# A depthwise convolution of 31 taps, with two more of its eight channel tiles on TensorE

## The chip, the cores and the metric

The kernel runs on one core of a Trainium2 chip. The metric is the device time of one execution in microseconds, as the median of several runs. TensorE (PE) multiplies matrices into PSUM, VectorE (DVE), ScalarE (ACT) and GpSimd (POOL) work elementwise, and SyncE (SP) issues most of the DMAs.

## The reference, cut to what matters

Two transformer blocks are computed in fp32 on a sequence of 512 positions of width 1024. The change lies in the convolution layer that opens the second block:

```python
def conformer_conv(x, norm_g, pw1_w, pw1_b, dw_w, dw_b, ln_g, ln_b, pw2_w, pw2_b):
    a, b = jnp.split(rmsnorm(x, norm_g) @ pw1_w + pw1_b, 2, axis=-1)
    h = a * jax.nn.sigmoid(b)
    h = lax.conv_general_dilated(h, dw_w[:, None, :], window_strides=(1,),
        padding=[(CONV_WIDTH - 1, 0)], feature_group_count=h.shape[-1], ...) + dw_b
    h = jax.nn.silu(layernorm(h, ln_g, ln_b))
    return h @ pw2_w + pw2_b
```

A first projection gives 2048 columns, whose halves are gated into 1024 channels. Each channel is filtered along the sequence by 31 taps of its own (causal: position s reads s-30 to s). Then come a layer norm over the channels, a SiLU and a second projection of 1024 columns.

## The kernel before

Activations lie transposed: a tile is 128 channels by 512 positions, so a layer has eight channel tiles, c = 0 to 7. The stage has four kinds of work.

**First projection.** `dense_g` (L259) makes one output tile after the other. Each fp32 product is three matmuls (`prod`, L228), with operands and weights split into a high and a low part; a tile takes 8 steps of 3 matmuls. Its weights come by DMA (`p_r`, SP's queue), are rounded on ACT (`p_h`, L223), and the rest is formed on DVE (`p_l`, L225). The opening group makes four tiles (the gates and values of c = 0 and 1) and lies before the code that is changed; twelve tiles follow, gate and value in turn for c = 2 to 7. A finished tile is read out of PSUM by DVE: a gate at L1196 (tile `sg`, then a sigmoid on ACT), a value at L1201 and L1202 (tile `gl`, the gated result). These products have three PSUM banks (`psm`), so a tile can't begin before the third one ahead of it has been read out.

**Filter on the elementwise engines** (`conv_taps`, L1259). On DVE a channel tile takes one multiplication (L1270) and 30 multiply-adds, one for each further tap (L1277, tile `dw`). With `two` set, ACT makes the 30 products instead (tile `dt`) and POOL adds them up (L1275). Before the change tiles 0 and 2 go the first way, one after the other, and tile 1 the second.

**Filter on TensorE** (`conv_start`, L1215, and `conv_pe`, L1243). Tiles 3 to 7 go this way. POOL builds two tiles `bd` of block-diagonal weights (L1223) from constants and taps alone. Four tiles `x4` hold shifted copies of the channel tile: 8 copies on ACT (L1236), 8 DMAs from SP's queue (L1238), after 4 small memsets on DVE (L1232). Then 8 groups of 4 matmuls, each 32 output columns wide, add up the taps (L1249). DVE reads the result out (L1254). For the last two tiles, 6 and 7, the same matmuls are in `close` (L1323), half of the sequence at a time, and DVE reads them out in `squares` (L1332, L1336).

**Layer norm.** After tile 0 is filtered, a matmul with ones takes its mean over 128 channels (L1288, tile `lnk`). This is subtracted from every tile to keep the sums of squares small. Each tile is added to a sum (L1303) and its square to another (L472). In `seam` (L300) the order is: `close(0)`, `squares(0)`, eight steps of `close(1)`, the statistics of the first half, its operands, the rest of `close(1)`, and so on; the second projection then begins. Because tile 6 has one PSUM bank, `close(1)` waits until `squares(0)` has read it.

**Order.** The streams are put in order by `Mix` (L88), with a clock of its own. A stream yields the time that it occupies TensorE and a delay until its next turn; among those that are ready the lowest rank goes first. The tap streams have rank 0 and 1, `conv_start` 10 + c, the projection 40 (0.65 for each step) and `conv_pe` 50. Only the projection, `lnk` and `conv_pe` move the clock, and `conv_pe` gets no turn before the projection is through. Each engine works its instructions off in one order fixed when the program is built. Activations share a pool of 72 slots.

Of the kernel before, what the change touches and what calls it, by code (L numbers as in the profile page):

```python
# [28 lines left out]
CMP = 31  # L29
NG = 8  # L30

C_PE, C_GP = 3, 1


C_ID, C_TRI, C_DM, C_LV = 0, 128, 256, 512
# [90 lines left out]
def body(ctx, tc, I, out, dump=None):  # L126
# [11 lines left out]
    def slot(name, dt=F32):  # L138
        return act.tile([P, S], dt, tag="s", name=name)
# [7 lines left out]
    def bank(name):  # L147
        return psg.tile([P, S], F32, tag="g", name=name)
# [16 lines left out]
    def af(o, i, func, **k):  # L165
        if func in (AF.Ln, AF.Exp):
            lnexp()
        elif func not in (AF.Copy, AF.Square):
            table[0] = func
        return A.activation(o, i, func, **k)  # L170
# [783 lines left out]
    mix = Mix()  # L954
# [299 lines left out]
            V.scalar_tensor_tensor(acc, ps, dwb[:, c:c + 1], sums["k"], ALU.add, ALU.subtract)  # L1254
            centred(c, acc)

    first = min(c for c in range(C_PE) if c != C_GP)

    def conv_taps(c, two, tap):  # L1259

        yield lambda: c in glu
        if two:
            yield 0.0, 16
        acc, t = slot(f"dw{c}"), glu[c]
        w = lambda d: dww[:, c, d:d + 1]
        if two:
            tmp = [slot(f"dt{c}_{i}") for i in range(5)]
            af(acc, t, AF.Identity, scale=w(0), bias=dwb[:, c:c + 1])
        else:
            V.tensor_scalar(acc, t, w(0), dwb[:, c:c + 1], ALU.mult, ALU.add)  # L1270
        for d in range(1, 31):
            if two:
                x = tmp[d % 5]
                af(x[:, d:], t[:, 0:S - d], AF.Copy, scale=w(d))
                G.tensor_tensor(acc[:, d:], acc[:, d:], x[:, d:], ALU.add)  # L1275
            else:
                V.scalar_tensor_tensor(acc[:, d:], t[:, 0:S - d], w(d), acc[:, d:], ALU.mult, ALU.add)  # L1277
            yield 0.0, tap
        return acc

    def conv_dve(two, cs, tap):
        for c in cs:
            acc = yield from conv_taps(c, two, tap)
            if c == first:

                yield 0.0, 4
                pk = bank("lnk")
                T.matmul(pk, ones, acc, start=True, stop=True)  # L1288
                k = slot("lnk")
                af(k, pk, AF.Copy, scale=1.0 / P)  # L1290
                sums["k"] = k
                yield 0.86, 1.25
            V.tensor_tensor(acc, acc, sums["k"], ALU.subtract)
            centred(c, acc)

    def centred(c, acc):
        cv[c] = acc
        if "s" not in sums:
            sums["s"] = slot("lns")
            V.tensor_copy(sums["s"], acc)  # L1300
            sums["q"] = Sq("lnq")
        else:
            V.tensor_tensor(sums["s"], sums["s"], acc, ALU.add)  # L1303
        sums["q"].add(acc)

    mix = Mix()
    mix.add(conv_dve(False, [c for c in range(C_PE) if c != C_GP], 1.2), 0)
    mix.add(conv_dve(True, [C_GP], 2), 1)
    for c in range(C_PE, KD):
        mix.add(conv_start(c), 10 + c)  # L1310
    mix.add(dense_g("p1", xs, pw1_groups, evacs["p1"], skip=1), 40)
# [377 lines left out]
    mix = Mix(2.5)  # L1689
# [108 lines left out]
```

## Time and profile before

| | |
|---|---|
| median of 3 runs (lowest, highest) | 2069.87 us (2067.83, 2072.08) |
| the profiled execution: time, span | 2069.71 us, 2067.9 us |
| PE busy | 1979.4 us, 96% of the span |
| DVE busy | 1575.2 us, 76% |
| ACT busy | 1032.5 us, 50% |
| POOL busy | 322.4 us, 16% |
| mean granted TensorE clock | 0.987 |

The time is that of the whole execution, and the span runs from the first to the last instruction. Shares are over the whole span; the convolution stage is about 130 us of it, from 893 to 1025 us.

### The profile page before, as it was taken

What the parts mean: (1) busy time and instruction counts of PE and PEld (TensorE: products, weight loads), DVE (VectorE), ACT (ScalarE), POOL (GpSimd) and SP (SyncE); (2) the same over time, 40 slices, a digit from 0 to 9 for tenths busy, and PEclk for the clock granted to TensorE, in tenths of its full rate; (3) what the DMA queues carried; (4) which work ended last, traced back from release to release, by engine and by line L of the source; (5) the groups of instructions that cost most, each with busy time, mean ns of one, the idle gap of its engine ahead of it and who ended that gap; (6) DMA issues with size and microseconds to landing.
All of it is one profiled execution on the core that took longest, in us unless ns stands there. A gap on an engine that the chain in (4) does not pass through costs nothing.

```text
span 2067.9 us, 31921 instructions
## 1 busy us (share of the span) xinstructions
PE 1979.4 (96%) x12400; PEld 1695.1 (82%) x12400; DVE 1575.2 (76%) x2914; ACT 1032.5 (50%) x1726; POOL 322.4 (16%) x225
## 2 busy tenths in 40 slices
PE   7898889999999999997799999999999999999998
PEld 5777777878899988885488999888766678999987
DVE  5888888655989972599978999634888868999832
ACT  5545666553544452456564445424756644444522
POOL 3332433101100000257000000000233310000000
PEclk9999999999999999998999999999999999999999
DMA  5221112312223333222122333324100022323332
GB/s 148 62 56 47 52 52 72 133 61 82 91 83 110 97 122 96 81 82 82 52 92 82 103 103 113 112 92 125 52 22 21 22 62 72 112 96 120 105 95 66
DMA packets 204190, 171.91 MB, mean 83 GB/s; under 512 B 13121, under 2 KB 198858, under 8 KB 204040
## 3 DMA queue, kind: packets, MB, share of 16 engines
q1 hardware_dynamic: 196864, 163.33, 25.5%
q10 hardware_dynamic: 6152, 3.40, 0.6%
q0 software_dynamic: 1024, 3.15, 0.4%
q8 instruction: 98, 1.61, 0.3%
q14 instruction: 52, 0.43, 0.1%
HBM read 165.15 MB, written 2.10 MB: 81 GB/s over the span
## 4 chain that ended last, share of the span: by engine, by line
PE 76%; DVE 18%; ACT 3%; issue 2%; DMA 1%; POOL 0%; ACTq 0%; DVEq 0%; SPq 0%; POOLq 0%
PE f L230 16%; PE f L232 16%; PE f L231 16%; DVE dw L1277 2%; PE ao L1676 2%; PE pT L1655 2%; DVE br L727 1%; DVE xc L728 1%; PE s L1568 1%; PE wo L230 1%; PE wo L232 1%; PE wo L231 1%; PE s L1566 1%; DVE p_l L225 1%; PE p L231 1%
## 5 line engine op out<-in xcount | busy, mean ns | idle before, releaser
L225 DVE TENSOR_TENSOR f_l<-f_r,f_h 128x1024 fp32r<-128x1024 f32 (+2 forms) x88 | 101.0, 1149 | 166.8 <-ACT f_h L223 166.3
L223 ACT CAST f_h<-f_r 128x1024 fp32r<-128x1024 f32 (+2 forms) x88 | 87.1, 992 | 188.4 <-PE f L231 148.7
L1646 POOL TENSOR_SCALAR p<-p,dn 128x256 f32<-128x256 f32 (+2 forms) x64 | 73.9, 1159 | 119.5 <-DVE dn L1644 87.3
L170 ACT ACTIVATE p<-s,nm 128x512 f32<-128x512 f32 (+3 forms) x128 | 66.2, 527 | 34.8 <-DVE nm L1640 13.9
L1442 POOL CAST KB<-K 128x128 fp32r<-128x128 f32 x4 | 1.6, 411 | 473.1 <-ACT K L1418 473.1
L1277 DVE SCALAR_TENSOR_TENSOR dw<-gl,dww,dw 128x511 f32<-128x511 f32 (+29 forms) x60 | 64.1, 1068 | 1.0
L170 ACT ACT_TABLE_LOAD x45 | 57.7, 1283 | 12.8 <-DVE v L644 4.9
L359 DVE TENSOR_TENSOR f_s<-f_s,f 128x1024 f32<-128x1024 f32 x52 | 63.3, 1218 | 0.1
L225 POOL TENSOR_TENSOR p_a_l<-p_a_r,p_a_h 128x1024 fp32r<-128x1024 f32 x4 | 9.9, 2474 | 330.3 <-DMA p_a_r<-in_a_pw_w 315.4
L1640 DVE TENSOR_REDUCE nm<-s 128x1 f32<-128x512 f32 (+2 forms) x96 | 50.1, 546 | 7.4 <-PE s L1568 6.7
L354 ACT CAST f_q1h<-f 128x1024 fp32r<-128x1024 f32 x26 | 27.3, 1051 | 55.8 <-DVE f_q3l L355 55.0
L1275 POOL TENSOR_TENSOR dw<-dw,dt 128x511 f32<-128x511 f32 (+29 forms) x30 | 47.1, 1571 | 33.0 <-ACT dt L170 31.1
L355 DVE TENSOR_TENSOR f_q1l<-f,f_q1h 128x1024 fp32r<-128x1024 f32 x26 | 31.9, 1225 | 24.9 <-ACT f_q1h L354 24.9
L1655 PEld LDWEIGHTS pT<-cst,p 128*128 128x128 f32 x320 | 36.0, 140 | 9.1 <-issue 4.2
L1676 PE MATMUL ao<-pt,vN 128*64 128x128 f32 (+3 forms) x256 | 42.6, 440 | 0.0
L354 ACT CAST f_q7h<-f 128x1024 fp32r<-128x1024 f32 x26 | 27.3, 1050 | 29.1 <-DVE f_q2l L355 26.6
L1655 PE MATMUL pT<-cst,p 128*128 128x128 f32 x320 | 41.0, 274 | 0.2 <-DVE pt L1659 0.2
L354 ACT CAST f_q2h<-f 128x1024 fp32r<-128x1024 f32 x26 | 27.4, 1054 | 27.6 <-issue 25.8
L727 DVE TENSOR_TENSOR br<-br,uc 128x4 f32<-128x4 f32 (+14 forms) x120 | 38.6, 321 | 2.5
L354 ACT CAST f_q5h<-f_s 128x1024 fp32r<-128x1024 f32 x26 | 27.3, 1052 | 26.3 <-DVE f_s L359 25.6
L354 ACT CAST f_q6h<-f_s 128x1024 fp32r<-128x1024 f32 x26 | 27.4, 1055 | 25.9 <-DVE f_s L359 21.5
L728 DVE TENSOR_TENSOR xc<-xc,br 128x4 f32<-128x4 f32 (+14 forms) x120 | 37.1, 309 | 2.7
(2420 smaller groups left out, 7963.2 us busy)
## 6 DMA issues: line engine op xcount, KB each, us to landing
f<-in_ffn_w_in SPq DMA_DIRECT2D x72, 512.0 KB, 3.9
f<-in_w_ffn_in SPq DMA_DIRECT2D x32, 512.0 KB, 3.5
f_r<-in_ffn_w_out SPq DMA_DIRECT2D x30, 512.0 KB, 3.4
p_r<-in_a_pw_w SPq DMA_DIRECT2D x20, 512.0 KB, 3.9
f_r<-in_w_ffn_out SPq DMA_DIRECT2D x14, 512.0 KB, 3.5
wo_r<-in_w_out SPq DMA_DIRECT2D x12, 512.0 KB, 3.4
f_r<-in_ffn_w_out SPq DMA_DIRECT2D x14, 384.0 KB, 3.1
wk_r<-in_gdn_w_in SPq DMA_DIRECT2D x8, 512.0 KB, 3.7
```

The source lines that it names most:

```text
L170: return A.activation(o, i, func, **k)
L223: A.copy(hi, raw)
L225: (G if idle else V).tensor_tensor(lo, raw, hi.bitcast(F32), ALU.subtract)
L230: T.matmul(ps, wh, xh, start=first, stop=False)
L231: T.matmul(ps, wh, xl, start=False, stop=False)
L232: T.matmul(ps, wl, xh, start=False, stop=last)
L354: A.copy(hi, raw)
L359: V.tensor_tensor(raws[o], raws[a], raws[b], ALU.add)
L1277: V.scalar_tensor_tensor(acc[:, d:], t[:, 0:S - d], w(d), acc[:, d:], ALU.mult, ALU.add)
L1646: (V if br else G).tensor_scalar(pp[br, qb], pp[br, qb], den[:, br:br + 1], None, ALU.mult)
L1655: T.transpose(ps[:, off + (qb - kb) * P:off + (qb - kb + 1) * P], bl(pp[br, qb], kb), ident)
L1676: T.matmul(po[64 * i:64 * i + 64, kb * P:S], VN[br][:, kb * P + 64 * g:kb * P + 64 * g + 64], rhs, start=False, stop=j == 7)
```

## The change

The constant that says how many tiles the elementwise engines filter goes from 3 to 1, and the one that names ACT's and POOL's tile goes. Only tile 0 stays, on DVE. Tiles 1 and 2 join tiles 3 to 5 in the loops over `range(C_PE, KD)` of `conv_start` and over `range(C_PE, KD - 2)` of `conv_pe`. The delay for a tap goes from 1.2 to 1.1. The branch for `two` stays in the code without a caller.

```diff
-C_PE, C_GP = 3, 1
+C_PE = 1
...
-    first = min(c for c in range(C_PE) if c != C_GP)
+    first = 0
...
     mix = Mix()
-    mix.add(conv_dve(False, [c for c in range(C_PE) if c != C_GP], 1.2), 0)
-    mix.add(conv_dve(True, [C_GP], 2), 1)
+    mix.add(conv_dve(False, range(C_PE), 1.1), 0)
     for c in range(C_PE, KD):
         mix.add(conv_start(c), 10 + c)
```

## Rows read from the trace of the kernel before

**Rows 1.** The page, part 1: engine, busy us (share), instructions.

```profile
PE 1979.4 (96%) x12400; PEld 1695.1 (82%) x12400; DVE 1575.2 (76%) x2914; ACT 1032.5 (50%) x1726; POOL 322.4 (16%) x225
```

**Rows 2.** Busy time by stretch: us, engines (instructions), granted clock, DMA.

```profile
893.06:936.80 43.74, 43.71 (x194) 35.86 (x192) 43.40 (x49) 23.09 (x32) 23.04 (x15) 1.00 0.37 107
936.80:954.10 17.30, 5.23 (x11) 3.39 (x12) 17.19 (x17) 7.71 (x12) 16.53 (x11) 0.58 0.21 65
954.10:975.59 21.49, 21.49 (x90) 17.02 (x88) 18.01 (x22) 17.47 (x29) 10.58 (x7) 0.94 0.37 98
975.59:995.65 20.06, 20.06 (x193) 6.26 (x196) 19.85 (x29) 13.67 (x22) 10.62 (x7) 1.00 0.31 89
995.65:1003.06 7.41, 7.41 (x132) 4.44 (x124) 7.22 (x11) 4.04 (x6) 0.00 (x0) 1.00 0.45 123
1003.06:1013.38 10.32, 0.00 (x1) 0.00 (x1) 10.12 (x17) 2.32 (x5) 0.00 (x0) 0.73 0.16 51
1013.38:1025.08 11.70, 10.61 (x133) 5.29 (x133) 7.64 (x20) 6.56 (x13) 0.00 (x0) 0.80 0.00 1
```

**Rows 3.** Waits of PE, 890 to 1030: us in total, times, longest.

```profile
PE cv L1328 <- DVE dw L1336: 10.3, 1, 10.3
PE lnk L1288 <- DVE x L1232: 8.6, 1, 8.6
PE p L230 <- DVE gl L1201: 3.5, 1, 3.5
```

**Rows 4.** PE in order of time, 890 to 1026: start, us, line, count, [idle before].

```profile
893.06 0.40 PE L230 MATMUL p<-f2x0h,p_h 128*128 128x512 f32 x1
...
931.17 0.39 PE L230 MATMUL p<-f2x0h,p_h 128*128 128x512 f32 x1
...
953.05 2.05 PE L1288 MATMUL lnk<-dw,ones 128*128 128x512 f32 x2 [8.59 <-DVE x L1232]
...
975.59 20.25 PE L1249 MATMUL cv<-x,bd 128*32 128x512 f32 x192
995.65 7.41 PE L1328 MATMUL cv<-x,bd 128*32 128x256 f32 x128
1013.38 5.96 PE L1328 MATMUL cv<-x,bd 128*32 128x256 f32 x64 [10.32 <-DVE dw L1336]
...
1020.33 3.66 PE L1328 MATMUL cv<-x,bd 128*32 128x256 f32 x64
```

**Rows 5.** DVE in order of time, 890 to 1015; columns as in rows 4.

```profile
890.67 6.05 DVE L225 TENSOR_TENSOR p_l<-p_r,p_h 128x1024 fp32r<-128x1024 f32 x3
...
904.34 3.09 DVE L1277 SCALAR_TENSOR_TENSOR dw<-gl,dww,dw 128x510 f32<-128x510 f32 x4
...
946.58 4.90 DVE L1277 SCALAR_TENSOR_TENSOR dw<-gl,dww,dw 128x485 f32<-128x485 f32 x3
951.40 0.68 DVE L1196 TENSOR_TENSOR sg<-p,f2nr 128x512 f32<-128x512 f32 x1
952.00 0.90 DVE L1277 SCALAR_TENSOR_TENSOR dw<-gl,dww,dw 128x482 f32<-128x482 f32 x1
...
1005.86 0.74 DVE L1254 SCALAR_TENSOR_TENSOR dw<-cv,vecs,lnk 128x512 f32<-128x512 f32 x1
```

**Rows 6.** DVE, line L225, 890 to 1015: count, ns min/median/max.

```profile
L225 DVE TENSOR_TENSOR p_l<-p_r,p_h x16: 1209/1222/2291, 890.7 to 1001.1; 128x1024 fp32r<-128x1024 f32 x16
```

**Rows 7.** POOL in order of time, 870 to 1042; columns as in rows 4.

```profile
890.42 7.20 POOL L1223 TENSOR_TENSOR bd<-rev,w 128x512 f32<-128x512 f32 x4
915.40 3.16 POOL L1275 TENSOR_TENSOR dw<-dw,dt 128x511 f32<-128x511 f32 x2 [17.78 <-ACT dt L170]
...
950.92 2.88 POOL L1223 TENSOR_TENSOR bd<-rev,w 128x512 f32<-128x512 f32 x2
```

**Rows 8.** ACT's copies for the shifted tiles: count, ns min/median/max, first and last start.

```profile
L1236 ACT COPY x<-gl x40: 602/617/622, 931.2 to 997.6; 32x512 f32<-32x512 f32 x20, 32x511 f32<-32x511 f32 x20
```

**Rows 9.** Groups by line, 985 to 1015: count, busy us, mean ns, idle before.

```profile
L1303 DVE TENSOR_TENSOR lns<-lns,dw 128x512 f32<-128x512 f32 x5 | 3.4, 687 | 0.0
```

## The prediction

> **What bounds the kernel now.** I read the page first. Over the whole span TensorE is busy 96% and VectorE 76% [rows 1], so the kernel looks bound by TensorE, and work moved onto TensorE should cost time. That share is an average over stages, so the second view is busy time by stretch of the convolution stage, and it says the opposite [rows 2]. From 893 to 1013 VectorE is busy in nearly all of every stretch, while TensorE works 5.2 us of 17.3 in one of them and not at all in another, with the granted clock at 0.58 and 0.73 there. The stage is bound by VectorE with gaps on TensorE. Third, the waits of TensorE name the gaps [rows 3]: 3.5 us for VectorE to read out a projection tile, 8.6 us in front of the matmul `lnk`, which needs tile 0 filtered, and 10.3 us in `seam`, where tile 6's bank must be read out. Fourth, TensorE in order of time [rows 4] gives the price of each piece, and VectorE and GpSimd in order of time [rows 5, 7] show why VectorE is late.
>
> The reason is in the taps. Four taps take 3.09 us with GpSimd idle, 0.77 each; three take 4.90, 1.63 each, while GpSimd adds up its own tile [rows 5, 7]. So GpSimd's help costs VectorE about what it saves.
>
> **What is removed.** Tile 2's 31 instructions on VectorE go, about 30 x 0.77 = 23 us and more where GpSimd was beside them; so do GpSimd's 30 additions and ACT's 31 products for tile 1. Their subtraction of the mean becomes a read-out of PSUM of like length (0.74 us) [rows 5]: nothing either way.
>
> **What TensorE gains at best.** Seven projection tiles take 931.17 - 893.06 = 38.11 us, 5.44 each, 0.68 for a step [rows 4]. Twelve without a stall, with some 0.5 us for `lnk` (1.05 at the slow clock, as two halves in 2.05 overlap), end at 893.06 + 65.3 + 0.5 = 958.9. They end at 975.6 now: 16.7 us lost, 12.1 of it the two waits [rows 3], 4.6 the lower clock behind them. In `seam` 10.3 us of waiting go, and the 64 records behind it, 5.96 us there, take 3.66 in the same form at full clock [rows 4]: 12.6 together. In all 29.3 us.
>
> **What TensorE gets on top.** Three filtered tiles run from 975.59 to 995.65 [rows 4], 6.69 us each, at granted clock 1.00 [rows 2]. Two more are 13.4 us. They lie on the path: `conv_pe` has the last rank and follows the whole projection, and `close` stands behind it. No part of them hides. The new balance is 29.3 - 13.4 = 15.9 us in hand, if VectorE is never late.
>
> A place where a rule and the row differ: the Trainium skill ("TensorE: Matmul & The Clock Gate", section "Part 3: Packing small matmuls — row/col tiling") has four tiles packed side by side run about three times as fast as one after the other. Taking its 3.07 on the 0.227 us of a full-width pass of the same length, a tile's 64 records would be an estimated 4.7 us, and the time 4 us lower than my sum. The row says 6.69, and the row is used.
>
> **What stays late.** The matmul `lnk` keeps its place. A tap waits 1.2 or now 1.1 of `Mix`'s clock, which moves in steps of 0.65, so both come to two projection steps; 30 taps are 60 steps, the delay of 4 is seven more. So `lnk` stands behind 67 steps, at 893.06 + 67 x 0.68 = 938.7 if nothing stalls, and it needs VectorE's chain for tile 0, which ended at 952.9 [rows 5]. In the same time GpSimd ran 26 instructions (4 from 890.42 on, 22 from 915.40 to the last row) [rows 7]. After the change it has only the `bd` tiles, 7 x 2 = 14, all with operands that are there at the start; I count all of them before `lnk`, as nothing else is in GpSimd's queue. That is 12 fewer. What one costs VectorE is bounded from both sides. Above: 1.63 - 0.77 = 0.86 us, from the taps. Below: without GpSimd VectorE would need, from 890.67, ten `p_l` x 1.22 [rows 6], eleven read-outs x 0.68, and 36 taps or instructions of that length x 0.77 [rows 5] = 47.4 us, to 938.1; the chain ended 14.8 us later, 0.57 for each of 26. (Durations overlap a little, so this end is low.) I take 0.77, nearer to the direct row: 12 x 0.77 = 9.2, the chain ends at 943.7, and TensorE waits 5.0 us at `lnk`; by the ends 3.9 to 7.4, and nothing if the fourteen fall where VectorE reads PSUM. The other wait (3.5) I count as gone: those read-outs come some 4 us earlier.
>
> A wait of this size costs clock too. After the two waits now, 4.6 us were lost, after the third 2.3 [rows 2, 4], so 2.3 each. Bounds 0 and 4.6; I take 2.3, since 3.5 us of idling already brought the clock to half.
>
> The Trainium skill ("SBUF — State Buffer", section "SBUF: two separate sides") says that a GpSimd instruction and a VectorE instruction with two SBUF inputs hold the shared ports one at a time, for the whole instruction. By that rule each of the 12 would give back the whole 0.86, and the wait would be 3.9, the time 1.1 us lower. The lockstep of rows 5 and 7 agrees; the mean over all 26 is lower, so I stay at 0.77.
>
> **What is hidden.** Two more sets of `x4` put 16 copies x 0.617 = 9.9 us on ACT [rows 8], less than the products that leave it, and 16 DMAs on SP's queue ahead of later weight loads. They come at steps 11 and 27. Behind the copies stand the rounding `p_h` and a sigmoid, for up to 5 us a set; those feed `p_l` and the gated tile, and TensorE needs `p_l` one tile later at the earliest. With three or four units of weights in the buffers that is covered by the 5.44 us tiles ahead; without that cover each set costs up to 5 us. The read-outs of five filtered tiles cost VectorE 0.74 + 2 x 0.69 = 2.1 us for each [rows 5, 9], beside 6.69 us of matmuls. Behind `seam` nothing changes.
>
> **The sum.** 2069.7 (the profiled execution, 0.2 below the median of 2069.9) - 29.3 + 13.4 + 5.0 + 2.3 = 2061.1 us, 8.6 faster.
>
> **Rivals.**
> *VectorE in time for `lnk`*: no new wait, 15.9 us faster, 2053.8. For it: VectorE alone would be ready at 938.1, against the place at 938.7. Against it: the first four `bd` did slow three `p_l` to 2.0 us each [rows 5, 6, 7]. Chance 0.2.
>
> *More late than that*: `x4` of tiles 1 and 2 on ACT and SP before the early weights, or 42 slots of 72 held by `bd` and `x4`, add 5 us of waiting. 2061.1 + 5 = 2066. Against it: the same sets for tiles 3 to 7 made no wait of TensorE on ACT or on a DMA in this stretch [rows 3]. Chance 0.16.
>
> *The wait moves to the read-out of PSUM, slower*: VectorE still reaches `squares(0)` late, as it now does, with read-outs of seven TensorE tiles in place of five. Then the 12.6 us stay and the sum is 2073.7. It decides from 6.3 us of waiting there, with the 2.3 of clock. The Trainium skill ("TensorEngine Tiling (Array Packing)", section "PSUM Bottleneck") warns that packing speeds up TensorE and not the reading of PSUM, which may then be the limit. Against it: 2.1 us of reading beside 6.69 us of matmuls, and VectorE has shed over 30 us. Chance 0.08.
>
> *The clock doesn't last through a longer filter stretch*: it would be 33.4 + 7.4 + 3.7 = 44.5 us, and at half clock 5.96/3.66 times that, 28 us more: 2089. Slower from 14 us at half clock on. Against it: 27 us of the same matmuls ran at 1.00 [rows 2]. Chance 0.04.
>
> **How the numbers follow.** The forecast has 0.52, with its own range 2057 to 2065. A measurement of this kernel tells 0.2%, 4.1 us, from no change: faster is below 2065.7. The forecast is faster in 0.48 of its 0.52, the first rival wholly, the second in half: 0.76. Within 0.2%: 0.04 + 0.08 + half of the slower read-out, 0.04 = 0.16. Slower: 0.08. The range runs from 2053.5, the first rival, to 2068, past the second.
>
> **What would show it.** Right: filter matmuls for five tiles in some 33 us at clock 1.00; a wait of 4 to 7 us before `lnk`; none before the second part of `close`; taps of 0.77 us from about 915 on; the `bd` tiles done by then. Wrong: TensorE waiting for ACT's copies or a weight DMA early in the projection, GpSimd's `bd` spread up to 950, a filter tile of other than 6.7 us, or a low clock in the filter stretch.

## The result and the profile after

The changed kernel takes 2058.12 us, the median of four runs (2056.20 to 2060.31), against 2070.38 (2067.83 to 2072.08): a ratio of 0.994 [0.9924, 0.9956], 12.3 us faster. The forecast was 2061.1 with a range of 2053.5 to 2068.0. The profiled execution is the longest of the four, 2060.31 us with a span of 2058.5 and a mean granted clock of 0.992, and its convolution stage begins 2.19 us later than before (895.25 against 893.06), behind code that is the same in both. So the stage is measured by itself below, from the first matmul of the twelve projection tiles to the first of the second projection. It took 132.02 us and takes 121.00.

The page, part 1 (engine, busy us, share, instructions):

```profile
PE 1989.4 (97%) x12528; PEld 1698.2 (82%) x12528; DVE 1534.8 (75%) x2891; ACT 1022.7 (50%) x1711; POOL 282.0 (14%) x199
```

Against [rows 1] TensorE has 128 instructions and 10.0 us more to do, and the kernel is faster: the share of TensorE over the whole span was the wrong thing to read.

Busy time by stretch of the changed kernel: length, PE, PEld, DVE, ACT and POOL (instructions), granted clock, DMA share, GB/s:

```profile
895.25:941.99 46.74, 45.82 (x203) 37.46 (x201) 46.42 (x65) 27.68 (x39) 19.03 (x13) 1.00 0.50 135
941.99:945.20 3.21, 0.89 (x4) 0.37 (x3) 3.17 (x9) 1.45 (x3) 0.00 (x0) 0.94 0.51 170
945.20:966.91 21.71, 21.71 (x89) 17.20 (x87) 10.27 (x21) 19.10 (x29) 0.00 (x0) 0.93 0.57 161
966.91:1000.34 33.43, 33.43 (x322) 10.43 (x325) 11.14 (x19) 9.67 (x16) 0.00 (x0) 1.00 0.19 54
1000.34:1010.44 10.10, 10.10 (x197) 6.11 (x189) 4.78 (x9) 2.75 (x4) 0.00 (x0) 1.00 0.01 2
1010.44:1016.25 5.81, 4.72 (x73) 2.66 (x69) 5.57 (x15) 4.46 (x10) 0.00 (x0) 1.00 0.01 3
```

In [rows 2] VectorE was full to 1013 and TensorE stood still twice. Now VectorE is full only until `lnk` has run (46.42 of 46.74, 3.17 of 3.21). In the filter it works 11.14 us of 33.43, and TensorE has every microsecond of that stretch and the next, at clock 1.00. GpSimd does nothing after the first row.

Waits of TensorE in the stage (releaser, us in total, times, longest):

```profile
PE lnk L1288 <- DVE x L1232: 2.3, 1, 2.3
...
PE p L230 <- ACT lx0h L1357: 1.1, 1, 1.1
PE p L230 <- DVE sg L1196: 0.9, 1, 0.9
```

The 10.3 us at `close(1)` of [rows 3] are gone, the 8.6 at `lnk` are 2.3, the 3.5 for the read-out of a value tile are gone, and a wait of 0.9 for the read-out of a gate tile is new. The wait of 1.1 for the operands of the second projection was there before too (1.08 ahead of the row at 1025.08) and is in the versions below.

TensorE in order of time (start, us, line, count, idle before):

```profile
895.25 0.40 PE L230 MATMUL p<-f2x0h,p_h 128*128 128x512 f32 x1
...
912.67 0.47 PE L230 MATMUL p<-f2x0h,p_h 128*128 128x512 f32 x1 [0.92 <-DVE sg L1196]
...
944.48 1.70 PE L1288 MATMUL lnk<-dw,ones 128*128 128x512 f32 x2 [2.33 <-DVE x L1232]
...
946.41 0.63 PE L231 MATMUL p<-f2x3l,p_h 128*128 128x512 f32 x1
...
966.91 33.61 PE L1249 MATMUL cv<-x,bd 128*32 128x512 f32 x320
1000.34 10.17 PE L1327 MATMUL cv<-x,bd 128*32 128x256 f32 x192
...
1016.25 0.74 PE L230 MATMUL p<-lx0h,p_h 128*128 128x256 f32 x4 [1.09 <-ACT lx0h L1357]
```

Beside [rows 4] the last three rows are the change: 320 filter records in place of 192, then 192 records of `close` without a break where 128 and 64 stood on both sides of 10.32 us. A matmul behind `lnk` takes 0.63 us, against 0.39 to 0.40 in [rows 4]: after a wait of 2.33 us TensorE is at the lower of its two levels (1.2 of 2.4 GHz; the granted clock is 0.50 from 946.41 to 948.00 and 1.00 again from 949.50), and the stretch as a whole has 0.93.

VectorE in order of time, and GpSimd's only row (same columns), each from the changed kernel:

```profile
908.40 2.06 DVE L225 TENSOR_TENSOR p_l<-p_r,p_h 128x1024 fp32r<-128x1024 f32 x1
...
917.44 2.30 DVE L1277 SCALAR_TENSOR_TENSOR dw<-gl,dww,dw 128x505 f32<-128x505 f32 x3
...
943.62 0.71 DVE L1277 SCALAR_TENSOR_TENSOR dw<-gl,dww,dw 128x482 f32<-128x482 f32 x1
...
1000.59 0.75 DVE L1254 SCALAR_TENSOR_TENSOR dw<-cv,vecs,lnk 128x512 f32<-128x512 f32 x1 [4.54 <-PE cv L1249]
1003.86 0.48 DVE L1335 SCALAR_TENSOR_TENSOR dw<-cv,vecs,lnk 128x256 f32<-128x256 f32 x1 [1.12 <-PE cv L1327]
```

```profile
892.62 21.67 POOL L1223 TENSOR_TENSOR bd<-rev,w 128x512 f32<-128x512 f32 x14
```

The fourteen `bd` tiles lie at the start. A `p_l` beside them takes 2.06 us (1.22 by the median of [rows 6]), and behind them three taps take 2.30, 0.77 each. Tile 0's chain ends at 944.33. In the last two rows of VectorE it now waits for TensorE, which is the reverse of [rows 3].

### The profile page after: what moved, and what is told of

The parts are those of the page before. It is cut to its first block, busy times and chain, and to the rows that moved or that the text cites. A ratio compares the mean times of both kernels' runs of the same rounds, so it can differ in the third digit from the quotient of the medians.

```text
span 2058.5 us, 32134 instructions
## 1 busy us (share of the span) xinstructions
PE 1989.4 (97%) x12528; PEld 1698.2 (82%) x12528; DVE 1534.8 (75%) x2891; ACT 1022.7 (50%) x1711; POOL 282.0 (14%) x199
## 4 chain that ended last, share of the span: by engine, by line
PE 78%; DVE 16%; ACT 3%; issue 2%; DMA 1%; POOL 1%; ACTq 0%; DVEq 0%; POOLq 0%
PE f L232 16%; PE f L230 16%; PE f L231 16%; PE ao L1675 2%; PE cv L1249 2%; PE pT L1654 2%; DVE br L727 1%; DVE xc L728 1%; PE p L231 1%; PE p L232 1%; PE p L230 1%; PE s L1567 1%; PE wo L230 1%; PE wo L231 1%; PE wo L232 1%
## 5 line engine op out<-in xcount | busy, mean ns | idle before, releaser
L225 DVE TENSOR_TENSOR f_l<-f_r,f_h 128x1024 fp32r<-128x1024 f32 (+2 forms) x88 | 101.2, 1152 | 166.6 <-ACT f_h L223 162.7
L225 POOL TENSOR_TENSOR p_a_l<-p_a_r,p_a_h 128x1024 fp32r<-128x1024 f32 x4 | 9.9, 2474 | 330.3 <-DMA p_a_r<-in_a_pw_w 315.4
L225 DVE TENSOR_TENSOR p_l<-p_r,p_h 128x1024 fp32r<-128x1024 f32 x20 | 28.1, 1415 | 13.4 <-ACT p_h L223 13.4
L359 DVE TENSOR_TENSOR f_s<-f,f 128x1024 f32<-128x1024 f32 x26 | 31.7, 1218 | 7.0 <-DMA f<-in_ffn_w_in 6.8
```

The costliest lines, as they stand in the source:

```text
L225: (G if idle else V).tensor_tensor(lo, raw, hi.bitcast(F32), ALU.subtract)
L359: V.tensor_tensor(raws[o], raws[a], raws[b], ALU.add)
```

## The experiments

The stage falls into three parts: the projection with `lnk` (to the first filter matmul), the filter (to `close(0)`), and the rest. Each row is one profiled execution, with the kernel's median, its ratio to the kernel before (measured beside it on the same chip, where that had medians of 2068.88 to 2070.38 us; 95% interval), and where the eight tiles are filtered.

| kernel | on VectorE; on TensorE | projection | filter | rest | stage | time | ratio |
|---|---|---|---|---|---|---|---|
| before | 0, 2 (1 on ACT and POOL); 3-7 | 82.53 | 20.06 | 29.43 | 132.02 | 2070.38 | |
| the change | 0; 1-7 | 71.66 | 33.43 | 15.91 | 121.00 | 2058.12 | 0.994 [0.9924, 0.9956] |
| the change again | 0; 1-7 | 71.67 | 33.42 | 15.91 | 121.00 | 2060.02 | 0.9951 [0.9937, 0.9964] |
| `e1_tile2_only` | 0 (1 on ACT and POOL); 2-7 | 82.14 | 26.74 | 15.91 | 124.79 | 2062.22 | 0.9968 [0.9959, 0.9978] |
| `e8_tile1_only` | 0, 2; 1, 3-7 | 68.36 | 26.74 | 15.91 | 111.01 | 2047.27 | 0.9897 [0.988, 0.9913] |
| `e2_two_on_dve` | 0, 1; 2-7 | 68.54 | 26.75 | 15.90 | 111.19 | 2048.71 | 0.9906 [0.9891, 0.9921] |
| `e3_three_on_dve` | 0, 1, 2; 3-7 | 67.02 | 20.07 | 42.06 | 129.15 | 2068.35 | 0.9993 [0.9983, 1.0003] |
| `e4_lnk_late` | as the change | 67.45 | 33.42 | 15.91 | 116.78 | 2053.76 | 0.993 [0.9915, 0.9945] |
| `e6_bd_after_lnk` | as the change | 66.31 | 33.42 | 15.91 | 115.64 | 2053.51 | 0.9928 [0.9913, 0.9942] |
| `e7_gp_busy` | as the change | 97.78 | 33.43 | 15.91 | 147.12 | 2085.12 | 1.0073 [1.0059, 1.0087] |
| `e5_two_dve_lnk_late` | 0, 1; 2-7 | 66.28 | 26.74 | 18.04 | 111.06 | 2047.98 | 0.9898 [0.9885, 0.991] |
| `e9_two_dve_bd_late` | 0, 1; 2-7 | 66.30 | 26.75 | 15.90 | 108.95 | 2046.48 | 0.9887 [0.9872, 0.9901] |

The theory was that of the prediction: each GpSimd instruction beside the taps costs VectorE 0.57 to 0.86 us, so the gain comes from taking work off GpSimd, and each tile that goes to TensorE costs 6.69 us on the path. The main rival was that VectorE's own load decides (tile 2), with GpSimd harmless beside it.

### The change again

> The changed kernel once more, beside the others of this call and in more rounds, for a narrower ratio. The ratio to the kernel before was 0.994 [0.9924, 0.9956]; both theories expect it again, 11 to 13 us faster.

Each part of the stage comes out the same to 0.01 us, while the median differs by 1.9 us (2060.02): the stage is the finer measure of the two.

### Each half of the change alone

Only tile 2 goes to TensorE; GpSimd keeps tile 1 (on the kernel before):

```diff
-C_PE, C_GP = 3, 1
+C_PE, C_GP = 2, 1
```

> Only tile 2 goes to TensorE; tile 1 stays on ACT and GpSimd. Measured so far: the stage, from the first matmul of the twelve projection tiles to the first of the second projection, takes 132.0 us before and 121.0 after the change. Theory A (GpSimd's additions beside VectorE's taps make the chain for tile 0 late; tile 2's taps make VectorE late at the end): the loss at lnk stays, 16.7 us, since the additions stay; the wait in seam goes, 13.5; one more filtered tile costs 6.7. Stage 132.0 - 13.5 + 6.7 = 125.2, time about 2063.5. Theory B (VectorE's own load with two tiles is the whole cause): the loss at lnk goes too, stage about 111 to 114, time about 2050.

The stage is 124.79 against the 125.2 that the theory gave. The 13.5 us of the rest come back, the filter grows by 6.68, and the projection stays at 82.14. Its waits, and the filter and `close` in order of time:

```profile
PE p L232 <- DVE p_l L225: 7.7, 2, 4.1
PE lnk L1288 <- DVE x L1232: 2.0, 1, 2.0
```

```profile
974.92 26.93 PE L1249 MATMUL cv<-x,bd 128*32 128x512 f32 x256
1001.66 10.17 PE L1328 MATMUL cv<-x,bd 128*32 128x256 f32 x192
```

VectorE's chain for tile 0 ends 59.22 us after the start of the stage, 59.84 before, so it is as late as it was, but now TensorE meets that at `p_l`, the low parts of the weights, instead of at `lnk`.

Only tile 1 goes to TensorE; tiles 0 and 2 stay on VectorE (on the changed kernel):

```diff
-        for c in range(C_PE, KD - 2):
+        for c in (1, 3, 4, 5):
...
-    mix.add(conv_dve(False, range(C_PE), 1.1), 0)
-    for c in range(C_PE, KD):
+    mix.add(conv_dve(False, (0, 2), 1.1), 0)
+    for c in (1, 3, 4, 5, 6, 7):
```

> Exactly one half of the change: tile 1 goes from ScalarE and GpSimd to TensorE, tiles 0 and 2 stay on VectorE. Theory A (GpSimd beside VectorE was the cause of both waits): as with tiles 0 and 1 on VectorE, stage 111 to 112 us, time about 2049; tile 2's move, the other half, is then a loss of some 10 us. Theory B (each half removes the wait that stands next to it, tile 1 the one at lnk, tile 2 the one in seam): the wait in seam stays, stage 121.0 - 6.7 + 13.5 = 128, time about 2065.

111.01 us, as the theory had it and 17 from its rival. In order of time:

```profile
940.62 1.10 PE L1288 MATMUL lnk<-dw,ones 128*128 128x512 f32 x2 [1.82 <-DVE x L1232]
...
961.40 26.93 PE L1249 MATMUL cv<-x,bd 128*32 128x512 f32 x256
988.14 10.17 PE L1327 MATMUL cv<-x,bd 128*32 128x256 f32 x192
```

No wait is left in `close` though VectorE keeps two tiles. So taking tile 1 off GpSimd and ScalarE is worth 132.02 - 111.01 = 21.0 us of the stage, and moving tile 2 as well loses 121.00 - 111.01 = 10.0 of it again: 6.69 of filter and 3.30 of projection. Tile 2's move by itself was worth 132.02 - 124.79 = 7.2 us (above): it pays only as long as GpSimd's tile is there.

### Two and three tiles on VectorE, none on GpSimd

```diff
-C_PE = 1
+C_PE = 2
```

> The changed kernel with C_PE = 2: tiles 0 and 1 on VectorE one after the other, nothing of the filter on GpSimd but the bd tiles, 2 to 7 on TensorE. Theory A: without GpSimd a second tile is 30 x 0.77 = 23 us, and in the changed kernel VectorE is idle for some 33 of the 60 us from 940 to 1000, so it fits; TensorE has one filtered tile less. Stage 121.0 - 6.7 = 114.3, time about 2051.5, faster than the change. Theory B: with two tiles on VectorE it is late again in front of squares(0), some 13 us come back: stage 121.0 - 6.7 + 13 = 127, time about 2064.

111.19, nearer to the theory (114.3) than to the rival (127). The theory's figure is the change's less one tile, 121.00 - 6.69; beyond that the projection loses 3.1 us less, 0.92 of it a wait that the change has and this version has not (below). TensorE, and VectorE at the second tile's taps and the read-out of the last tile of `conv_pe`:

```profile
941.80 1.10 PE L1288 MATMUL lnk<-dw,ones 128*128 128x512 f32 x2 [2.02 <-DVE x L1232]
942.97 0.39 PE L231 MATMUL p<-f2x3l,p_h 128*128 128x512 f32 x1
...
962.58 26.93 PE L1249 MATMUL cv<-x,bd 128*32 128x512 f32 x256
```

```profile
977.85 4.51 DVE L1277 SCALAR_TENSOR_TENSOR dw<-gl,dww,dw 128x487 f32<-128x487 f32 x6
...
989.58 0.75 DVE L1254 SCALAR_TENSOR_TENSOR dw<-cv,vecs,lnk 128x512 f32<-128x512 f32 x1 [2.40 <-PE cv L1249]
```

A wait of 2.02 us left the next matmul at 0.39, full speed, and the granted clock at 1.00 from there to 950; the 2.33 of the change was followed by 0.63. With two tiles VectorE still waits 2.40 us for TensorE ahead of `squares`.

With `C_PE = 3` all three tiles of the kernel before are on VectorE, without GpSimd's help:

> The changed kernel with C_PE = 3: tiles 0, 1 and 2 on VectorE, nothing of the filter on GpSimd but the bd tiles. Theory A: 46 us more for VectorE than in the change, where 33 are free, while TensorE would be through 13.4 us earlier: VectorE is late by about 26 us, stage 121.0 - 13.4 + 26 = 134, time about 2071, as before the change or a little slower. If GpSimd had helped before, in spite of the slow taps, this must be clearly slower than before, by 10 us and more (theory B).

The theory had 134 us of stage and 2071, the rival clearly slower than before. The stage measures 129.15, 4.9 below the theory and 2.9 below the kernel before, and the time of 2068.35 is that of the kernel before (0.9993). TensorE, and VectorE with tile 2's taps:

```profile
1011.30 5.27 PE L1327 MATMUL cv<-x,bd 128*32 128x256 f32 x64 [24.34 <-DVE dw L1335]
```

```profile
986.31 23.08 DVE L1277 SCALAR_TENSOR_TENSOR dw<-gl,dww,dw 128x511 f32<-128x511 f32 x30
```

The thirty taps take 23.08 us, and TensorE waits 24.34 for them in one place, where the kernel before waited 22.4 in three [rows 3]. The tile on ACT and GpSimd was worth nothing.

### What one GpSimd instruction costs

Thirty additions of 512 columns on GpSimd beside tile 0's chain; their result is not read (on the changed kernel):

```diff
+    gd = slot("gd"); G.memset(gd, 0.0)
+    def extra():
+        for d in range(1, 31):
+            G.tensor_tensor(gd[:, d:], gd[:, d:], hT[0][:, d:], ALU.add)
+            yield 0.0, 1.1
+    mix.add(extra(), 1)
```

> The changed kernel with 30 more GpSimd additions of the old length (512 columns) on a tile that nothing reads, put beside the taps of tile 0; VectorE, ScalarE and TensorE have the same work. Theory A: each that falls beside the chain costs 0.6 to 0.9 us, 20 to 30 of them 12 to 27 us; the wait at lnk is 15 to 29 us, time 2072 to 2088. Rival (VectorE's own load was the cause): no change, 2058.

2085.12, slower than the kernel before. Waits of TensorE, and one stretch of GpSimd:

```profile
PE p L230 <- DVE sg L1196: 8.8, 3, 5.5
PE lnk L1288 <- DVE x L1232: 7.4, 1, 7.4
PE p L230 <- DVE gl L1201: 5.3, 2, 2.8
```

```profile
920.13 30.96 POOL L1311 TENSOR_TENSOR gd<-gd,f2v 128x499 f32<-128x499 f32 x18
```

Tile 0's chain ends 74.76 us after the start of the stage, against 49.08 in the change: 25.7 us for 30 instructions, 0.86 each. The theory had the delay at `lnk`; most of it (14.1 of 21.5) is at read-outs of projection tiles, since those stand behind the taps in VectorE's queue. An addition with VectorE idle beside it (the last one, where only tile 2 has moved) lasts 1.22 us by the profile, whose spans on GpSimd are rough: by that an addition costs VectorE less than its own length.

The reverse: the `bd` tiles are built only after tile 0's mean is there, by way of a zero made from that mean:

```diff
+        yield lambda: "k" in sums
+        if "rev" not in sums:
+            z = const.tile([P, 1], ...)
+            af(z, sums["k"][:, 0:1], AF.Copy, scale=0.0)
+            sums["rev"] = const.tile([P, 32], ...)
+            af(sums["rev"], rev[:, 32:64], AF.Identity, bias=z)
+        # the loop over q2 that builds bd stands here, on sums["rev"], behind the x4 tiles
```

> The changed kernel with GpSimd's fourteen bd tiles made after lnk: their constants go through a copy that takes a zero from the mean, so GpSimd is idle during the taps of tile 0. lnk keeps its place behind 67 steps. Theory A (each GpSimd instruction beside the taps delays VectorE, by 10.8 us / 12 = 0.9 by the two traces): the chain for tile 0 ends up to 12 us earlier after the start of the stage (49.1 us now), as far as the projection lets it; both waits of the projection (0.9 and 2.3 us) and the lower clock go; time about 2053. Rival (what held VectorE up there was its own queue, not GpSimd): chain and time as in the change, 2058, or slower, if the filter on TensorE must wait for bd.

2053.51, as expected. TensorE at `lnk`, VectorE's last tap and GpSimd's `bd`:

```profile
937.15 1.02 PE L1294 MATMUL lnk<-dw,ones 128*128 128x512 f32 x2
```

```profile
932.87 0.71 DVE L1283 SCALAR_TENSOR_TENSOR dw<-gl,dww,dw 128x482 f32<-128x482 f32 x1
```

```profile
940.90 18.30 POOL L1243 TENSOR_TENSOR bd<-rev,w 128x512 f32<-128x512 f32 x14 [51.94 <-ACT rev L170]
```

Both waits of the projection, the 2.33 and the new 0.92, are gone, and 66.31 us is its floor (65.3 + 0.5 by the prediction). The chain ends 42.02 us after the start: the fourteen `bd` cost it 7.06 us, 0.50 each, or a little more, since VectorE now waits 1.3 us itself ahead of the chain. That is less than an addition's price; several of them run before the chain has begun, or beside read-outs of PSUM.

### The place of `lnk`

Its delay behind tile 0's last tap goes from 4 to 10 of the planner's units:

```diff
-                yield 0.0, 4
+                yield 0.0, 10
                 pk = bank("lnk")
```

> The changed kernel with the delay ahead of the matmul lnk at 10 in place of 4, so that it stands behind 76 steps of the projection in place of 67, 6.1 us later, when tile 0 is ready. Theory A (the wait of 2.3 us there and the lower clock behind it are pure loss): both go, 2.3 + 1.9 = 4.2 us, time about 2054. Rival (the wait only moves, or VectorE, which takes the mean from lnk, becomes late): no change, 2058, or slower.

2053.76, as expected for a wait that goes. `lnk` stands later and without a wait:

```profile
943.71 1.02 PE L1288 MATMUL lnk<-dw,ones 128*128 128x512 f32 x2
```

The stage is 4.22 us shorter: the wait of 2.33 and 1.9 of clock. The wait of 2.33 us was paid almost twice. By the time alone this isn't shown, since the intervals of this version and of the change overlap.

The same delay with two tiles on VectorE (`C_PE = 2`):

> The changed kernel with tiles 0 and 1 on VectorE (C_PE = 2) and the delay ahead of lnk at 10. Measured so far: tiles 0 and 1 on VectorE 2048.7, where 2.0 us of waiting at lnk were left; lnk later 2053.8 against 2058.1 for the change. Theory A: the gains add up but for what the first has taken of the second already: 2.0 us less, and the clock stayed high there, so 2046 to 2047. Rival: tile 1's taps start 6 us later behind a later lnk, VectorE is late in front of squares(0) and some 5 us come back: 2051 to 2054.

Half a miss. The wait at `lnk` goes and the projection is at its floor (66.28), but the stage is 111.06, as without the delay. VectorE at the subtraction of the mean, and TensorE in `close(1)`:

```profile
956.24 0.69 DVE L1293 TENSOR_TENSOR dw<-dw,lnk 128x512 f32<-128x512 f32 x1 [5.15 <-ACT lnk L170]
```

```profile
995.92 3.66 PE L1327 MATMUL cv<-x,bd 128*32 128x256 f32 x64 [1.92 <-DVE dw L1335]
```

What was won at `lnk` is waited for in `close(1)`: VectorE waits 5.15 us for the mean, all that needs it was put off, and it reaches `squares(0)` late.

### Both together

`bd` behind the mean, as above, and `C_PE = 2`:

> Tiles 0 and 1 on VectorE (C_PE = 2) and the twelve bd tiles after lnk, beside tile 1's taps in place of tile 0's. Theory A: the 2.0 us at lnk go, but the twelve now delay tile 1's taps by 0.5 to 0.9 us each, 6 to 11 us; VectorE had no time left in front of squares(0) with two tiles (0 to 2 us), so a wait of 4 to 9 us comes there: stage 111.2 - 2.0 + 4 to 9 = 113 to 118, time 2051 to 2056. Rival (contention matters only where a chain is short of time, and there is none): 2046.5.

The theory missed: it had the `bd` tiles slow tile 1's taps so that a wait of 4 to 9 us comes ahead of `squares(0)`. The rival's 2046.5 came. TensorE, VectorE at the end of tile 1's chain and in `squares`, and GpSimd:

```profile
938.33 1.02 PE L1294 MATMUL lnk<-dw,ones 128*128 128x512 f32 x2
...
959.04 26.93 PE L1255 MATMUL cv<-x,bd 128*32 128x512 f32 x256
985.79 10.17 PE L1333 MATMUL cv<-x,bd 128*32 128x256 f32 x192
```

```profile
984.44 0.71 DVE L1283 SCALAR_TENSOR_TENSOR dw<-gl,dww,dw 128x482 f32<-128x482 f32 x1
...
991.10 0.48 DVE L1341 SCALAR_TENSOR_TENSOR dw<-cv,vecs,lnk 128x256 f32<-128x256 f32 x1
```

```profile
942.07 18.16 POOL L1243 TENSOR_TENSOR bd<-rev,w 128x512 f32<-128x512 f32 x12 [51.93 <-ACT rev L170]
```

The chain is later, as expected (it ends at 985.15, 92.4 us after the start, against 88.3 with the `bd` tiles at the start), but VectorE had slack: the 2.40 us shown for two tiles on VectorE, and more in `squares`. Its first read-out there comes 991.10 - 985.79 = 5.3 us after `close(0)` begins, against 3.5 with the `bd` tiles at the start, and that is still ahead of `close(1)`: `close` runs its 192 records without a break. All three parts are at their floors, 66.30, 26.75 and 15.90. At 2046.48 us this is the fastest median here; its interval [0.9872, 0.9901] overlaps those of the other versions with two tiles on VectorE, so that it beats them is shown by the stage alone (108.95 against 111.01 to 111.19). Against the change it is 11.6 us faster, and the intervals lie apart.

## Why the prediction was right

**The bound** was read rightly: VectorE, held up by GpSimd. Three versions show it from three sides: GpSimd's tile taken away alone gives 21.0 us of stage, its work put on VectorE costs nothing, and thirty additions put back lose 26.1. The first two take ACT's products away as well; the third touches GpSimd alone.

**The gain at best.** 29.3 us were counted. By the floors it is 82.53 - 66.30 = 16.2 in the projection (16.7 counted) and 29.43 - 15.91 = 13.5 behind the filter (12.6): 29.7 together. The wait in `seam` went wholly, as counted.

**The two filtered tiles.** 33.43 - 20.06 = 13.37 us (13.4), at clock 1.00 through all 33 us. None of it is hidden, and the rival of a falling clock is out. A tile is 33.43 / 5 = 6.69 us. The 4.7 us that the prediction estimated from the Trainium skill's 3.07 ("TensorE: Matmul & The Clock Gate", "Part 3: Packing small matmuls — row/col tiling") was not met, but its base was wrong. The 3.07 is measured there for four row tiles, and the 0.227 us that it was put on is a pass of the projection, whose operands are rounded. The filter's are plain fp32, as those of `lnk`, whose two records of 512 columns take 1.02 us at full clock and 0.59 each (a filter record of 512 columns lasts 0.60): the second starts 0.43 behind the first. Against 0.43 the filter's 33.43 / 320 = 0.104 us for a record is about four times as fast, an estimate from these rows.

**The wait at `lnk`** was the term that was mis-sized: 5.0 counted, 2.33 measured. Two parts of it moved. `lnk`'s place came 46.90 us after the start, not 45.6, of which 0.92 is the new wait below; the count of 67 steps held (937.15 - 891.56 = 45.59 where nothing stalls). And the chain ended 49.08 us after the start, not 50.6: 59.84 - 49.08 = 10.76 us were given back, not 9.2.

The mistake in the 9.2 was to charge one price for two kinds of instruction. Between the rows of [rows 7] GpSimd ran, before the change:

```profile
918.53 2.93 POOL L1223 TENSOR_TENSOR bd<-rev,w 128x512 f32<-128x512 f32 x2
921.42 3.39 POOL L1275 TENSOR_TENSOR dw<-dw,dt 128x509 f32<-128x509 f32 x2
927.27 8.32 POOL L1275 TENSOR_TENSOR dw<-dw,dt 128x507 f32<-128x507 f32 x5 [2.46 <-ACT dt L170]
935.54 3.46 POOL L1223 TENSOR_TENSOR bd<-rev,w 128x512 f32<-128x512 f32 x2
938.97 11.99 POOL L1275 TENSOR_TENSOR dw<-dw,dt 128x502 f32<-128x502 f32 x7
```

The 26 were sixteen additions and ten `bd`. After the change they are fourteen `bd`: sixteen additions went and four `bd` came, which the prediction counted as twelve fewer. Without GpSimd the chain takes 42.02 us, so the 26 cost 59.84 - 42.02 = 17.82 us, 0.69 each; the lower bound of 0.57 came out low because it put the chain alone at 45.0. If a `bd` cost 0.50 before as well, an addition cost (17.82 - 10 x 0.50) / 16 = 0.80, an estimate, and 16 x 0.80 - 4 x 0.50 = 10.8 is what was given back. So the 0.77 was near the price of an addition, and the count of twelve was what made the sum short.

The Trainium skill ("SBUF — State Buffer", "SBUF: two separate sides") has a GpSimd instruction that reads SBUF and a VectorE instruction with two SBUF inputs lock each other out for the whole instruction; by that rule the forecast would have been 1.1 us lower, as it said. The trace agrees in part. A read-out of PSUM, which has one input in SBUF, keeps its 0.68 us beside a `bd` (951.40 in [rows 5], 950.92 in [rows 7]). But a tap beside an addition takes 1.63 us, and the two alone would be 0.77 + 1.22 = 1.99 with the rough span above, so that the lock lasts for the whole of an addition isn't shown.

**The clock behind it**: 2.3 counted. The projection lost 71.66 - 66.31 = 5.35 us in all; without the two waits, 2.33 and 0.92, that leaves 2.10.

**What I did not see**: the wait of 0.92 us for `sg`. The fourteen `bd` tiles now stand together at the start, where they slow `p_l` (2.06 us) and so delay the read-out behind it. It is gone where `bd` comes after the mean, and also in the versions with a tile fewer on TensorE, which have twelve `bd`. The rivals of waiting for ACT's copies or the early weights, and for the read-out of PSUM, did not come.

**The sum.** The stage was forecast 8.6 us shorter and is 11.0 shorter. The difference of 2.4 is 2.7 for the wait at `lnk`, 0.9 for `seam` and 0.2 for the clock, less 0.9 for the new wait and 0.5 by which the projection had less to win. What the prediction did not ask is whether both tiles should move: tile 1 was enough.

**Open.** Why the granted clock stayed up after waits of 1.82 and 2.02 us and not after 2.33 (2.29 when the change ran again) was not tried apart from the rest. The first matmuls behind a wait don't tell it: with thirty additions on GpSimd a wait of 2.96 us was followed by 1.3 us of matmuls at 0.39 to 0.47, and only then by 0.63:

```profile
942.15 0.47 PE L230 MATMUL p<-f2x0h,p_h 128*128 128x512 f32 x1 [2.96 <-DVE sg L1196]
...
943.42 0.63 PE L232 MATMUL p<-f2x1h,p_l 128*128 128x512 f32 x1
```

Nor was a `bd` timed alone, so its 0.50 mixes instructions beside the chain with others ahead of it.

## What to carry to other kernels

Read the bound stage by stage: an engine at 96% of the span can still be the one to which work should go, if in the stage at hand it waits for another. Work given to GpSimd beside a busy VectorE has to be charged to VectorE, at what the trace shows for the two together and for each kind of instruction by itself, before it is called help. When a balance is moved, try each part of the move alone, since here one half alone won 21.0 us of the stage, the other alone 7.2, and both together 11.0.

## What the runs showed of the hardware

Thirty GpSimd additions of 512 columns beside VectorE's multiply-adds cost VectorE 25.7 us, 0.86 each, more than the 0.77 that VectorE takes for such a multiply-add itself; the tile on ACT and GpSimd against the same tile on VectorE came to 0.9993 [0.9983, 1.0003]. A read-out of PSUM kept its 0.68 us beside GpSimd's work. Four matmuls of 32 columns side by side kept the clock at 1.00 for 33 us, with 6.69 us for 64 records. A wait of TensorE of 2.33 us cost about 2 us more behind it, in matmuls at 0.63 us and a granted clock of 0.93 over the next 21.7 us; a wait of 2.02 us was followed by matmuls of 0.39 us at a granted clock of 1.00.
